# A two-layer hybrid encoder on Trainium2: the scan's output decay factors are loaded with its other loads, and four out-projection steps are written behind the last third's splits

## The chip, the cores and the metric

The kernel runs on one core of one Trainium2 chip, as one program. The metric is the device time of one execution in microseconds (us); the time of a kernel is the median of its runs. One core has a matrix engine (TensorE, PE; its weight loads are listed apart as PEld), a vector engine (VectorE, DVE), a scalar engine (ScalarE, ACT), GpSimd (POOL), and SyncE (SP), which here only issues transfers (DMAs). Each engine works through its own instructions in the order in which they stand, and waits where one needs what another engine or a transfer has not delivered. On-chip data lies in tiles; a pool of tiles under one tag has a fixed number of buffers, and a new tile waits until the last user of its buffer is done. Results of TensorE lie in PSUM banks until another engine has read them.

## The reference

Two layers, 1040 tokens (1024 and 16 meta tokens) of width 1024. Each layer: RMSNorm, one input projection to four groups of mixers (pooling, 2-D Fourier, a bidirectional state-space scan called SSD, attention) and their gates, one output projection, and the residual. The change lies in the scan and in the output projection of its group. The scan, cut to its core:

```python
def ssd_direction(xh, dt, a, bm, cm):
    ...
    da = (dt * a).reshape(b, nc, CHUNK, SSD_GROUPS, r).transpose(0, 1, 3, 4, 2)
    cs = jnp.cumsum(da, axis=-1)
    seg = cs[..., :, None] - cs[..., None, :]
    lmat = jnp.exp(jnp.where(lower, seg, -jnp.inf))
    cb = jnp.einsum("bclgn,bcsgn->bcgls", cc, bc)
    y_diag = jnp.einsum("bcgrls,bcsgrp->bclgrp", cb[:, :, :, None] * lmat, xdt)
    decay_to_end = jnp.exp(cs[..., -1:] - cs)
    chunk_states = jnp.einsum("bclgn,bcgrl,bclgrp->bcgrpn", bc, decay_to_end, xdt)
    ...
    _, prev = lax.scan(step, h0, (chunk_states, chunk_decay))
    y_off = jnp.einsum("bclgn,bcgrpn,bcgrl->bclgrp", cc, prev, jnp.exp(cs))
    return (y_diag + y_off).reshape(b, lp, nh, p)

def ssd_mixer(...):
    ...
    y = (y_fwd + y_bwd)[:, META_PAD:] + d_skip.astype(jnp.float32)[:, None] * xh
    y = y.reshape(b, n, W_SSD) * jax.nn.silu(z.astype(jnp.float32))
    return rmsnorm(y, norm_w).astype(out_dtype)
```

The kernel works with chunks of 104 tokens (QC), so 10 chunks (NQ) for a layer. The factors exp(cs) in `y_off` are what the kernel keeps under the name `ecd`; the cumulative sums for `lmat` are under `csd`.

## The kernel before

All is written as generators that yield after each piece, and a `weave` takes from several of them in proportion, so that the order on each engine is the order in which the pieces were written. Tokens are cut into three thirds of about 348, 346 and 346 columns (the last layer leaves the meta tokens out: 332, 346, 346; chunks 0, 1 and 2 in `ssd_fin` and `outproj`; "third" below, so as not to mix them with the scan's chunks).

The forward part of the scan is `ssd_fwd`. For scan chunk q, `prepare(q)` (P0 to P9 below) loads two broadcast tiles of cumulative sums, `rf` and `rb` (L868, L869, 338 KB each), from the pool `bb` with NBB = 5 buffers; the masks' products are L880 and L881 on VectorE; eight times L883 on VectorE and an Exp on ScalarE make the decays; eight times L887 on ScalarE and L888 on VectorE add the backward part; L889 on GpSimd multiplies both into `rb`. `finish(q)` (F0 to F9) takes a tile `e` from the pool `big`, loads the output decay factors into it with two transfers from `ecd` (L897), multiplies the products with the backward and forward states into it (L900, L903 on VectorE from PSUM; the matmuls are L825), updates the state (`ssd_state`: L808 on VectorE, L811 on TensorE, L817 on GpSimd, L818 on VectorE), adds both directions (L908 on GpSimd), does the products within the chunk (L914, 16 matmuls), adds them (L915) and writes y with the skip (four L917 on VectorE). The order is P0, P1, F0, P2, F1 and so on to P9, F8, F9: `prepare` runs one chunk ahead.

Where a third is complete, `ssd_fin` multiplies it with the gate z (loaded in L945; L950 on VectorE), sums the squares (L952 on ScalarE, L954 on VectorE) and yields; behind that yield come the sum over partitions on TensorE (L957), the root (L142 to L145) and the scaling (L961 on VectorE). `ssd_parts` then splits y into a high and a low part (L128 on ScalarE, L129 on VectorE), the two operands of the three-matmul products (L132 to L134). The same `split` is used on weights (`wl<-wr,wh`).

The scan is woven with other work: its first FW = 17 pieces with steps of the output projection of the attention group, its last 5 with `tail((0, 1))`, the out-projection of the scan's own group for thirds 0 and 1. That has 16 steps (8 output tiles d by 2 thirds; k0 to k15 below). A step loads the residual (`sms<-hd`, L338), runs 12 matmuls into PSUM `psmm`, adds the result to the residual on VectorE (L352), and stores it (L353). In this stage `psmm` has two banks. TW = 20 stands for 16 steps, so the weave writes them at four to a piece of the scan. Behind it comes `rest`, the same for the last third: its splits, and 8 steps. In the last layer `rest` runs alone; in the first it is woven with the next layer's input norm. SyncE issues all loads and stores named here, in order.

Of the kernel before, what the change touches and what calls it, by code (L numbers as in the profile page):

```python
# [52 lines left out]
def hybrid_trunk(ctx: ExitStack, tc: tile.TileContext, io, out, depth=DEPTH):  # L53
    nc = tc.nc
# [15 lines left out]
    nc.vector.memset(ones, 1.0)  # L70
    epst = const.tile([128, 1], F32, name="epst")
    nc.vector.memset(epst, EPS)
    FW, TW = 17, 20
    NBIG, NBB = 30, 5
    WB = (4, 5)
    PB, KB, NPF, NACC = 2, 3, 14, 4
    SPARE = (('xx', 'xx', 'mm'), ('sc', 'sc', 'mm'), ('xx', 'mm', 'xx'), ('xx', 'sc', 'xx'))
# [19 lines left out]
    def big(dt=F32):  # L97
        return bigp.tile([128, SLOT], dt, name=nm("big"), tag="big", bufs=NBIG)
# [758 lines left out]
    def ssd_fwd(l, s):  # L857
# [5 lines left out]
        def prepare(q):  # L863

            qs = slice(q * QC, (q + 1) * QC)
            tok = s.tok[q]
            rf, rb = vr(bb()[:QC]), vr(bb()[:QC])
            nc.sync.dma_start(rf, s.csd[q, 0].partition_broadcast(QC))  # L868
            nc.sync.dma_start(rb, s.csd[q, 1].partition_broadcast(QC))  # L869
            px, bt = ssd_tok(s, q)  # L870
            xx = big()
            xt, xw = xx[:QC, :512], xx[:QC, 512:1024]
            nc.scalar.copy(xt, px[:QC])
            pc = ps("xx")
            for g in range(2):
                nc.tensor.matmul(pc[:QC, g * QC:(g + 1) * QC], s.xbc[4 + g][:, qs], s.xbc[6 + g][:, qs], start=True, stop=True)
            cfb = phase["p"].tile([128, 4 * QC], F32, name=nm("cfb"), tag="cfb", bufs=1)[:QC].rearrange("p (g t) -> p g t", t=QC)
            cf, cb = cfb[:, 0:2], cfb[:, 2:4]
            pcv = pc[:QC, :2 * QC].rearrange("p (g t) -> p g t", t=QC)
            nc.vector.tensor_tensor(cf, pcv, mf.unsqueeze(1).broadcast_to([QC, 2, QC]), op=ALU.mult)  # L880
            nc.vector.tensor_tensor(cb, pcv, mb.unsqueeze(1).broadcast_to([QC, 2, QC]), op=ALU.mult)  # L881
            for r in range(8):
                nc.vector.scalar_tensor_tensor(rf[:, r], rb[:, r], s.gap[:, q, r:r + 1], rf[:, r], op0=ALU.add, op1=ALU.min)  # L883
                nc.scalar.activation(rf[:, r], rf[:, r], AF.Exp, bias=tok[:, r:r + 1])
            for r in range(8):
                g = (r % 4) // 2
                nc.scalar.activation(rb[:, r], cb[:, g], AF.Copy, scale=tok[:, 136 + r:137 + r])  # L887
                nc.vector.scalar_tensor_tensor(rb[:, r], cf[:, g], tok[:, 104 + r:105 + r], rb[:, r], op0=ALU.mult, op1=ALU.add)  # L888
            nc.gpsimd.tensor_tensor(rb, rb, rf, op=ALU.mult)  # L889
            ready[q] = (xt, xw, bt, rb)  # L890

        def finish(q, st):
            qs = slice(q * QC, (q + 1) * QC)
            xt, xw, bt, rb = ready.pop(q)
            e = vr(big())
            for a in range(2):
                nc.sync.dma_start(e[64 * a:64 * a + 64].rearrange("p (i j) t -> p i j t", i=2), s.ecd[q, :, 4 * a:4 * a + 4].partition_broadcast(64))  # L897
            if q < NQ - 1:
                pb = ssd_off(s, q, s.sb[q], "sc")
                nc.vector.tensor_tensor(e[:, 4:8], pb.rearrange("p (j t) -> p j t", t=QC), e[:, 4:8], op=ALU.mult)  # L900
            if q > 0:
                pf = ssd_off(s, q, st, "pv")
                nc.vector.tensor_tensor(e[:, 0:4], pf.rearrange("p (j t) -> p j t", t=QC), e[:, 0:4], op=ALU.mult)  # L903
            new = None
            if q < NQ - 1:
                new = ssd_state(s, 0, q, xt, bt, st, xw, s.sf[:, 512 * (q % 2):512 * (q % 2) + 512])
            if 0 < q < NQ - 1:
                nc.gpsimd.tensor_tensor(e[:, 0:4], e[:, 0:4], e[:, 4:8], op=ALU.add)  # L908
            y = e[:, 4:8] if q == 0 else e[:, 0:4]
            pd = ps("xx")  # L910
            for h in range(8):
                j, a = h // 2, h % 2
                r = 4 * a + j
                nc.tensor.matmul(pd[64 * a:64 * a + 64, j * QC:(j + 1) * QC], xt[:, h * 64:h * 64 + 64], rb[:, r], start=True, stop=True)  # L914
            nc.vector.tensor_tensor(y, y, pd[:, :4 * QC].rearrange("p (j t) -> p j t", t=QC), op=ALU.add)  # L915
            for j in range(4):
                nc.vector.scalar_tensor_tensor(s.y[j][:, qs], s.xbc[j][:, qs], vec(l, V_DS + j), y[:, j], op0=ALU.mult, op1=ALU.add)  # L917
            return new
# [3 lines left out]
        for q in range(NQ + 1):  # L922
# [7 lines left out]
            if q:  # L930
                st = finish(q - 1, st)
                ci = next((i for i, (c0, cw) in enumerate(CH) if (q - 1) * QC < c0 + cw <= q * QC), None)
                if ci is not None:
                    norm = ssd_fin(l, s, ci)
                    next(norm)
                yield
        next(norm, None)
        yield

# [38 lines left out]
    def run(*gens):  # L978
        for g in gens:
            for _ in g:  # L980
                pass
# [41 lines left out]
    for l in range(depth):  # L1023
# [59 lines left out]
        stage(bwd, 5, FB[7])  # L1083
        hsrc = by_rows(out, NM) if last else hidden()
        sink = None if last else []
        tail = lambda chunks: outproj(l, s, 2, lambda: ssd_parts(s, chunks), d1, hsrc, chunks, sink=sink)
        fwd = ssd_fwd(l, s)
        n = 48 - FB[6] - FB[7]
        stage(islice(fwd, FW), FW, n)
        run(weave((fwd, 22 - FW), (tail((0, 1)), TW)))  # L1090
        scope.close()
        rest = tail((2,))
        if last:
            run(rest)
        else:
# [109 lines left out]
```

## Time and profile before

| | before |
|---|---|
| three runs, median (lowest to highest) | 2136.37 us (2135.49 to 2142.13) |
| the profiled execution | 2144.23 us |
| its span in the profile | 2142.5 us |
| mean granted clock of TensorE | 0.969 |
| scan of layer 0, forward, up to F9 | about 825 to 1062 us of the span |
| forward scan of layer 1, up to F9 | up to 2114 us of the span |

The page of a profile lists engines with busy time and share, then groups of instructions. A group or a row of the timeline reads: start, duration, engine, line, operation, output tile, inputs, and in brackets how long the engine stood idle before it and what released it. A window's row lists the busy time of each engine in a stretch of time, the granted clock of TensorE (1.00 is full), and the share of the transfer engines in use. Times in rows count from the start of the span. A transfer is named by its tiles (`big<-ecd`). Records of successive instructions overlap a little, by some 0.08 us on VectorE.

### The profile page before, as it was taken

What the parts mean: (1) busy time and instruction counts of PE and PEld (TensorE: products, weight loads), DVE (VectorE), ACT (ScalarE), POOL (GpSimd) and SP (SyncE); (2) the same over time, 40 slices, a digit from 0 to 9 for tenths busy, and PEclk for the clock granted to TensorE, in tenths of its full rate; (3) what the DMA queues carried; (4) which work ended last, traced back from release to release, by engine and by line L of the source; (5) the groups of instructions that cost most, each with busy time, mean ns of one, the idle gap of its engine ahead of it and who ended that gap; (6) DMA issues with size and microseconds to landing.
All of it is one profiled execution on the core that took longest, in us unless ns stands there. A gap on an engine that the chain in (4) does not pass through costs nothing.

```text
span 2142.5 us, 33401 instructions
## 1 busy us (share of the span) xinstructions
PE 2007.5 (94%) x11880; PEld 1756.2 (82%) x11880; DVE 1398.6 (65%) x2785; ACT 1012.6 (47%) x2191; POOL 464.2 (22%) x465
## 2 busy tenths in 40 slices
PE   6999999999999898888889999999999998979888
PEld 5898988688899568877779988877888995878878
DVE  5575547767664455689795655476675635476996
ACT  5534344453542546356464344435534433463652
POOL 2012122031110210245230221221311103012550
PEclk9999999999999999999999999998999999988999
DMA  4322222123233477676643221212223344776666
GB/s 138 99 74 62 64 63 57 43 76 97 91 127 104 135 210 246 193 187 191 169 123 116 66 67 54 73 44 72 68 98 102 117 129 127 241 217 180 175 184 195
DMA packets 164605, 261.01 MB, mean 122 GB/s; under 512 B 20878, under 2 KB 113618, under 8 KB 164438
## 3 DMA queue, kind: packets, MB, share of 16 engines
q1 hardware_dynamic: 161782, 249.55, 38.7%
q0 software_dynamic: 2656, 9.33, 1.8%
q8 instruction: 93, 1.52, 0.3%
q14 instruction: 74, 0.61, 0.1%
HBM read 182.91 MB, written 71.67 MB: 119 GB/s over the span
## 4 chain that ended last, share of the span: by engine, by line
PE 68%; DVE 14%; DMA 9%; ACT 4%; issue 3%; POOL 2%; SPq 1%; DVEq 0%; POOLq 0%; ACTq 0%
PE psmm L132 11%; PE psmm L133 10%; PE psmm L134 10%; PE pspv L678 6%; PE psy L132 5%; PE psy L133 5%; PE psy L134 5%; PE psy L655 2%; PE psy L626 2%; PE psy L656 2%; DMA hd<-sms 2%; DVE bb L883 1%; PE pssc L655 1%; DMA big<-ecd 1%; PE pssc L626 1%
## 5 line engine op out<-in xcount | busy, mean ns | idle before, releaser
L132 PE MATMUL psmm<-big,wh 128*128 128x346 f32 (+2 forms) x1920 | 645.5, 337 | 42.0 <-DVE sms L352 19.2
L133 PE MATMUL psmm<-big,wh 128*128 128x346 f32 (+2 forms) x1920 | 633.8, 330 | 7.6 <-DVE big L129 4.7
L134 PE MATMUL psmm<-big,wl 128*128 128x346 f32 (+2 forms) x1920 | 628.2, 327 | 1.3 <-DVE wl L129 1.3
L132 PEld LDWEIGHTS psmm<-big,wh 128*128 128x128 f32 x1920 | 370.8, 193 | 88.0 <-issue 29.3
L133 PEld LDWEIGHTS psmm<-big,wh 128*128 128x128 f32 x1920 | 371.0, 193 | 17.8 <-DVE big L129 7.2
L134 PEld LDWEIGHTS psmm<-big,wl 128*128 128x128 f32 x1920 | 371.3, 193 | 4.5 <-DVE wl L129 2.4
L668 POOL TENSOR_TENSOR acc<-acc,pf 116x346 f32<-116x346 f32 (+5 forms) x216 | 222.9, 1044 | 701.2 <-ACT pf L658 557.4
L128 ACT CAST wh<-wr 128x512 fp32r<-128x512 f32 (+1 forms) x236 | 145.2, 616 | 268.6 <-PE psmm L133 205.8
L129 DVE TENSOR_TENSOR wl<-wr,wh 128x512 fp32r<-128x512 f32 x232 | 168.4, 730 | 126.6 <-ACT wh L128 125.2
L132 PE MATMUL psy<-big,wh 128*128 128x346 f32 (+2 forms) x672 | 221.8, 330 | 1.1 <-ACT big L128 0.6
L133 PE MATMUL psy<-big,wh 128*128 128x346 f32 (+2 forms) x672 | 217.7, 324 | 3.1 <-DVE big L188 2.0
L134 PE MATMUL psy<-big,wl 128*128 128x346 f32 (+2 forms) x672 | 216.8, 323 | 0.0
L678 PE MATMUL pspv<-pf,vt 116*64 116x346 f32 (+5 forms) x864 | 168.8, 469 | 0.0
L658 ACT ACTIVATE pf<-psy 116x346 f32<-116x346 f32 (+4 forms) x288 | 125.3, 457 | 87.0 <-PE psy L656 84.8
L668 DVE TENSOR_TENSOR acc<-acc,pf 116x346 f32<-116x346 f32 (+5 forms) x120 | 106.7, 889 | 71.5 <-ACT pf L658 51.0
L627 DVE TENSOR_REDUCE mx<-psy 116x1 f32<-116x346 f32 (+3 forms) x272 | 132.7, 511 | 18.5 <-PE psy L626 18.0
L132 PEld LDWEIGHTS psy<-big,wh 128*128 128x128 f32 x672 | 127.2, 189 | 13.3 <-issue 7.6
L133 PEld LDWEIGHTS psy<-big,wh 128*128 128x128 f32 x672 | 127.0, 189 | 6.9 <-DVE big L188 3.1
L134 PEld LDWEIGHTS psy<-big,wl 128*128 128x128 f32 x672 | 127.0, 189 | 0.8
L678 PEld LDWEIGHTS pspv<-pf,vt 116*64 116x64 f32 (+1 forms) x864 | 59.4, 137 | 62.5 <-issue 26.7
L655 PE MATMUL psy<-big,big 128*116 128x346 f32 (+4 forms) x288 | 96.2, 336 | 0.9 <-DVE mx L627 0.8
L627 DVE TENSOR_REDUCE mx<-pssc 128x1 f32<-128x346 f32 (+3 forms) x136 | 69.8, 513 | 41.7 <-PE pssc L626 40.0
(293 smaller groups left out, 3326.7 us busy)
## 6 DMA issues: line engine op xcount, KB each, us to landing
wr<-w SPq DMA_DIRECT2D x248, 256.0 KB
sms<-hd SPq DMA_DIRECT2D x112, 173.0 KB
hd<-sms SPq DMA_DIRECT2D x96, 173.0 KB
bb<-csd SPq DMA_DIRECT2D x40, 338.0 KB
md<-big SPq DMA_DIRECT2D x24, 520.0 KB
gd<-sms SPq DMA_DIRECT2D x64, 173.0 KB
big<-gd SPq DMA_DIRECT2D x16, 520.0 KB
big<-md SPq DMA_DIRECT2D x16, 520.0 KB
```

The lines of the kernel that those rows point to most:

```text
L128: nc.scalar.copy(hi, src)
L129: nc.vector.tensor_tensor(lo, src, f(hi), op=ALU.subtract)
L132: nc.tensor.matmul(out_ps, ah, bh, start=start, stop=False)
L133: nc.tensor.matmul(out_ps, ah, bl, start=False, stop=False)
L134: nc.tensor.matmul(out_ps, al, bh, start=False, stop=stop)
L626: nc.tensor.matmul(p[:qn, :cw], s1[e][:, q0:q0 + qn], k1[:, c0:c0 + cw], start=True, stop=True)
L627: nc.vector.tensor_reduce(mx[:qn, q, e, ci:ci + 1], p[:qn, :cw], axis=AX.X, op=ALU.max)
L655: nc.tensor.matmul(p[:n, :cw], k1[:, k0:k0 + n], s1[e][:, cs], start=True, stop=False)
L656: nc.tensor.matmul(p[:n, :cw], k3[0:65, k0:k0 + n], q2[e][0:65, cs], start=False, stop=True)
L658: nc.scalar.activation(pf[:n, :cw], p[:n, :cw], AF.Exp, scale=0.125)
L668: eng.tensor_tensor(accs[c0, e][:n, :cw], accs[c0, e][:n, :cw], pf[:n, :cw], op=ALU.add)
L678: nc.tensor.matmul(hold["pv"][64 * e:64 * e + 64, :cw], s.vt[:n, k, v, :], pfs[e][:n, :cw], start=(k == 0), stop=(k == len(KTS) - 1))
```

## The change

There are three edits. First, `e` is taken from the pool `bb` and loaded in `prepare(q)`, right behind the loads of `rf` and `rb`, instead of in `finish(q)` from `big`; `bb` gets 7 buffers instead of 5 (three tiles a chunk instead of two). Second, `ssd_fwd` yields twice more, with no work, ahead of the last third's norm. Third, of the 16 steps of `tail((0, 1))` only the first 12 (TL) are woven with the last 7 pieces of the scan; then `ssd_parts` of the last third is written, then the remaining 4 steps (`run(front)`), and then `rest`, which takes the splits already written. The number of matmuls, products and transfers is the same.

Lines of the functions move by 3 and by 2: L880 becomes L883, L883 L886, L888 L891, L889 L892, L945 L947, L950 L952, L954 L956, L957 L959, L961 L963; L900 to L917 keep their numbers, and the load of e is L872 instead of L897.

```diff
@@ -70,8 +70,8 @@
     nc.vector.memset(ones, 1.0)
     epst = const.tile([128, 1], F32, name="epst")
     nc.vector.memset(epst, EPS)
-    FW, TW = 17, 20
-    NBIG, NBB = 30, 5
+    FW, TL = 17, 12
+    NBIG, NBB = 30, 7
     WB = (4, 5)
     PB, KB, NPF, NACC = 2, 3, 14, 4
     SPARE = (('xx', 'xx', 'mm'), ('sc', 'sc', 'mm'), ('xx', 'mm', 'xx'), ('xx', 'sc', 'xx'))
@@ -867,6 +867,9 @@
             rf, rb = vr(bb()[:QC]), vr(bb()[:QC])
             nc.sync.dma_start(rf, s.csd[q, 0].partition_broadcast(QC))
             nc.sync.dma_start(rb, s.csd[q, 1].partition_broadcast(QC))
+            e = vr(bb())
+            for a in range(2):
+                nc.sync.dma_start(e[64 * a:64 * a + 64].rearrange("p (i j) t -> p i j t", i=2), s.ecd[q, :, 4 * a:4 * a + 4].partition_broadcast(64))
             px, bt = ssd_tok(s, q)
             xx = big()
             xt, xw = xx[:QC, :512], xx[:QC, 512:1024]
@@ -887,14 +890,11 @@
                 nc.scalar.activation(rb[:, r], cb[:, g], AF.Copy, scale=tok[:, 136 + r:137 + r])
                 nc.vector.scalar_tensor_tensor(rb[:, r], cf[:, g], tok[:, 104 + r:105 + r], rb[:, r], op0=ALU.mult, op1=ALU.add)
             nc.gpsimd.tensor_tensor(rb, rb, rf, op=ALU.mult)
-            ready[q] = (xt, xw, bt, rb)
+            ready[q] = (xt, xw, bt, rb, e)
 
         def finish(q, st):
             qs = slice(q * QC, (q + 1) * QC)
-            xt, xw, bt, rb = ready.pop(q)
-            e = vr(big())
-            for a in range(2):
-                nc.sync.dma_start(e[64 * a:64 * a + 64].rearrange("p (i j) t -> p i j t", i=2), s.ecd[q, :, 4 * a:4 * a + 4].partition_broadcast(64))
+            xt, xw, bt, rb, e = ready.pop(q)
             if q < NQ - 1:
                 pb = ssd_off(s, q, s.sb[q], "sc")
                 nc.vector.tensor_tensor(e[:, 4:8], pb.rearrange("p (j t) -> p j t", t=QC), e[:, 4:8], op=ALU.mult)
@@ -934,6 +934,8 @@
                     norm = ssd_fin(l, s, ci)
                     next(norm)
                 yield
+        yield
+        yield
         next(norm, None)
         yield
 
@@ -1083,13 +1085,16 @@
         stage(bwd, 5, FB[7])
         hsrc = by_rows(out, NM) if last else hidden()
         sink = None if last else []
-        tail = lambda chunks: outproj(l, s, 2, lambda: ssd_parts(s, chunks), d1, hsrc, chunks, sink=sink)
+        tail = lambda chunks, parts: outproj(l, s, 2, parts, d1, hsrc, chunks, sink=sink)
         fwd = ssd_fwd(l, s)
         n = 48 - FB[6] - FB[7]
         stage(islice(fwd, FW), FW, n)
-        run(weave((fwd, 22 - FW), (tail((0, 1)), TW)))
+        front = tail((0, 1), lambda: ssd_parts(s, (0, 1)))
+        run(weave((fwd, 24 - FW), (islice(front, TL), TL)))
         scope.close()
-        rest = tail((2,))
+        ym = ssd_parts(s, (2,))
+        run(front)
+        rest = tail((2,), lambda: ym)
         if last:
             run(rest)
         else:
```

What moves on the engines, at three places. First SyncE, the tail of layer 0's scan: e of the last chunk (`big_10708`) before the change, between stores of the residual (`hd_8851`, `hd_8852`) and loads of weights (`wr`). A row is the line, the operation, the output and input tile with its buffer number, and the shape.

```order
L205 DMA wr_11043<-w 128x512
L205 DMA wr_11099<-w 128x512
L897 DMA big_10708<-ecd_3642 64x2x416
L353 DMA hd_8851<-big_10688 128x348
L353 DMA hd_8852<-big_10688 128x346
L897 DMA big_10708<-ecd_3642 64x2x416
L205 DMA wr_11131<-w 128x512
```

The same tile after the change (`bb_10441`), among the loads and stores of the residual (`sms<-hd`, `hd<-sms`) of the last attention steps:

```order
L868 DMA bb_10437<-csd_3641 104x832
L338 DMA sms_10182<-hd_5734 128x346
L338 DMA sms_10201<-hd_5735 128x346
L869 DMA bb_10438<-csd_3641 104x832
L947 DMA z_10608<-gd_6603 128x4x346
L353 DMA hd_5731<-sms_10182 128x346
L353 DMA hd_5732<-sms_10201 128x346
L338 DMA sms_10299<-hd_5733 128x348
L205 DMA wr_10818<-w 128x512
L338 DMA sms_10318<-hd_5734 128x346
L872 DMA bb_10441<-ecd_3642 64x2x416
```

The load has moved ahead of the whole tail, to the other loads of its chunk, and in front of residual loads and stores of attention steps.

Second VectorE, the tail of layer 1's scan, before: the evictions of the steps (L352) stand close together ahead of F9's first product (L903).

```order
L352 TENSOR_TENSOR sms_21509<-sms_21509,psmm_21511 128x332
L352 TENSOR_TENSOR sms_21526<-sms_21526,psmm_21528 128x346
L129 TENSOR_TENSOR wl_21775<-wr_21772,wh_21774 128x512
L352 TENSOR_TENSOR sms_21549<-sms_21549,psmm_21551 128x332
L352 TENSOR_TENSOR sms_21566<-sms_21566,psmm_21568 128x346
L129 TENSOR_TENSOR wl_21798<-wr_21795,wh_21797 128x512
L903 TENSOR_TENSOR big_21583<-pspv_21586,big_21583 128x416
```

The last two L352 above are those of steps k8 and k9. After the change, from the eviction of step k3 on:

```order
L352 TENSOR_TENSOR sms_21449<-sms_21449,psmm_21451 128x346
L915 TENSOR_TENSOR bb_21104<-bb_21104,psy_21435 128x416
L129 TENSOR_TENSOR wl_21548<-wr_21545,wh_21547 128x512
L818 TENSOR_TENSOR big_19757<-big_19757,pspv_21428 128x512
L917 SCALAR_TENSOR_TENSOR big_19073<-big_19073,vecs,bb_21104 128x104
L917 SCALAR_TENSOR_TENSOR big_19074<-big_19074,vecs,bb_21104 128x104
L917 SCALAR_TENSOR_TENSOR big_19075<-big_19075,vecs,bb_21104 128x104
L917 SCALAR_TENSOR_TENSOR big_19076<-big_19076,vecs,bb_21104 128x104
L129 TENSOR_TENSOR wl_21588<-wr_21585,wh_21587 128x512
L903 TENSOR_TENSOR bb_21320<-pspv_21466,bb_21320 128x416
L129 TENSOR_TENSOR wl_21643<-wr_21640,wh_21642 128x512
```

Evictions of the first four steps (k0 to k3) now stand ahead of the end of F8, and no other L352 stands among the rest of F8 and F9. The next one, that of k4, follows 24 rows behind that of k3.

Third VectorE, the same tail, around the last third's squares. Before (L954 sums the squares, L143 is the root's first step, behind the norm sum on TensorE; the L352 are of k10, k11 and k12):

```order
L954 TENSOR_TENSOR sms_21610<-sms_21610,smn_21618 128x346
L129 TENSOR_TENSOR wl_21821<-wr_21818,wh_21820 128x512
L954 TENSOR_TENSOR sms_21610<-sms_21610,smn_21622 128x346
L352 TENSOR_TENSOR sms_21631<-sms_21631,psmm_21633 128x332
L352 TENSOR_TENSOR sms_21648<-sms_21648,psmm_21650 128x346
L143 SCALAR_TENSOR_TENSOR smn_21711<-psy_21705,smn_21711 128x346
L352 TENSOR_TENSOR sms_21671<-sms_21671,psmm_21673 128x332
```

After (the sum is L956; the L352 are of k4 to k8):

```order
L956 TENSOR_TENSOR sms_21490<-sms_21490,smn_21494 128x346
L129 TENSOR_TENSOR wl_21735<-wr_21732,wh_21734 128x512
L956 TENSOR_TENSOR sms_21490<-sms_21490,smn_21498 128x346
L352 TENSOR_TENSOR sms_21511<-sms_21511,psmm_21513 128x332
L956 TENSOR_TENSOR sms_21490<-sms_21490,smn_21502 128x346
L352 TENSOR_TENSOR sms_21528<-sms_21528,psmm_21530 128x346
L352 TENSOR_TENSOR sms_21551<-sms_21551,psmm_21553 128x332
L352 TENSOR_TENSOR sms_21568<-sms_21568,psmm_21570 128x346
L129 TENSOR_TENSOR wl_21775<-wr_21772,wh_21774 128x512
L352 TENSOR_TENSOR sms_21591<-sms_21591,psmm_21593 128x332
L143 SCALAR_TENSOR_TENSOR smn_21614<-psy_21608,smn_21614 128x346
```

Between the last sum of squares and the root there stood two steps; now there are four, and seven steps in place of four follow the norm sum on TensorE.

## The prediction

> **What bounds the kernel now.** I read the page first, then busy time in windows of the scan and of the work behind it, then the waits of TensorE (PE) and VectorE (DVE) there. The page says whose time counts:
>
> ```profile
> PE 2007.5 (94%) x11880; PEld 1756.2 (82%) x11880; DVE 1398.6 (65%) x2785; ACT 1012.6 (47%) x2191; POOL 464.2 (22%) x465
> ```
>
> TensorE sets the span, so a gain has to come out of TensorE's waits or of its slow clock. In the changed stage it is more mixed. Columns of the windows: length, then busy us and count of PE, PEld, DVE, ACT, POOL, then granted clock, DMA share, GB/s.
>
> ```profile
> 960.00:980.00 20.00, 16.68 (x101) 14.53 (x101) 20.00 (x46) 15.51 (x40) 10.40 (x9) 0.93 0.70 180
> 1000.00:1020.00 20.00, 17.93 (x109) 16.82 (x109) 18.24 (x40) 12.90 (x36) 11.40 (x10) 0.83 0.69 195
> 2020.00:2040.00 20.00, 17.32 (x119) 15.72 (x118) 19.64 (x43) 13.62 (x33) 11.68 (x11) 0.91 0.56 153
> 2060.00:2080.00 20.00, 16.50 (x103) 15.10 (x102) 19.32 (x43) 12.88 (x37) 10.79 (x10) 0.83 0.72 194
> 1056.00:1062.00 6.00, 0.22 (x2) 0.00 (x0) 5.69 (x15) 2.35 (x5) 0.35 (x1) 0.75 0.47 128
> 1062.00:1066.00 4.00, 3.88 (x12) 3.40 (x13) 1.57 (x5) 2.26 (x6) 0.00 (x0) 0.52 0.63 149
> 2108.00:2114.00 6.00, 2.80 (x18) 2.51 (x17) 5.75 (x15) 2.25 (x5) 0.00 (x0) 0.97 0.76 251
> 2114.00:2117.00 3.00, 3.00 (x9) 2.52 (x10) 0.59 (x3) 1.53 (x3) 0.00 (x0) 0.50 0.77 228
> ```
>
> In the scan VectorE is busy 18.2 to 20.0 of 20 us while TensorE has holes and a clock of 0.83 to 0.93: VectorE is the bound there. At the scan's end (1056 to 1062, 2108 to 2114) TensorE stands while VectorE finishes, and then runs at half clock. Those two holes are what the held-back steps aim at. Their waits, with TensorE's short operations around them:
>
> ```profile
> 1046.55 1.10 PE L811 MATMUL pspv<-big,smq 104*128 104x256 f32 x4 [1.31 <-DVE big L903]
> 1062.12 1.52 PE L957 MATMUL psy<-sms,ones 128*128 128x346 f32 x2 [5.90 <-DVE sms L954]
> 2104.80 1.04 PE L825 MATMUL pspv<-big,big 128*128 128x104 f32 x8
> 2105.76 0.93 PE L914 MATMUL psxx<-bb,big 104*64 104x104 f32 x16
> 2113.80 1.52 PE L957 MATMUL psy<-sms,ones 128*128 128x346 f32 x2 [3.20 <-DVE sms L954]
> ```
>
> So 1.31 + 5.90 us in layer 0 and 3.20 us in layer 1. Behind each long one lies half clock: 4.0 us at 0.52 and 3.0 us at 0.50, about 1.9 and 1.5 us lost.
>
> **Part 1: e is loaded two chunks ahead.** VectorE's waits for it, and what GpSimd (POOL) and SyncE did there:
>
> ```profile
> 1000.78 0.59 DVE L900 TENSOR_TENSOR big<-pssc,big 128x416 f32<-128x416 f32 x1 [1.56 <-DMA big<-ecd]
> 1045.31 0.59 DVE L900 TENSOR_TENSOR big<-pssc,big 128x416 f32<-128x416 f32 x1 [2.37 <-DMA big<-ecd]
> 1051.50 0.58 SPq L897 DMA_DIRECT2D big<-ecd  x1
> 1055.83 0.59 DVE L903 TENSOR_TENSOR big<-pspv,big 128x416 f32<-128x416 f32 x1 [4.08 <-DMA big<-ecd]
> 2010.49 1.06 POOL L908 TENSOR_TENSOR big<-big 128x416 f32<-128x416 f32 x1
> 2011.59 0.59 DVE L915 TENSOR_TENSOR big<-big,psxx 128x416 f32<-128x416 f32 x1 [1.42 <-POOL big L908]
> ```
>
> All of these but the last name a DMA that SyncE issued late, behind stores of the residual; F9's second half was issued at 1051.50 and used at 1055.83. After the change no use of e waits. What is late next differs. In layer 0's scan (1000.78) VectorE goes on at once with ready work: I take 0.9 of the 1.56 us (nothing to 1.56 are the ends; GpSimd's add, 1.06 us as in the row of 2010.49, follows e and takes part back). In layer 1's scan VectorE's next wait is for that add, itself behind GpSimd's queue, so an earlier e saves about nothing. The waits at 1045.31 and 1055.83 belong to the tail, summed below as a whole. Three tiles of bb a chunk on seven buffers instead of two on five cost no instruction, but move the slot waits: rf of chunk k now waits for the last L917 of chunk k-3, where it waited for its L914 matmuls, and e of chunk k for the L914 of chunk k-2. From L914's start at 2105.76 to the end of its L917 (2108.91 + 1.04, below) are 4.2 us, from L914's end 3.3 us. SyncE works in order, and behind the waiting DMA stand residual loads (L338) and stores (L353) of the attention steps. I set this against the just-in-time e loads that no longer stand in front of the tail's stores: nothing net, between -3 us and the loss of the second rival.
>
> **Part 2: fewer steps woven in, four held back.** A step is 12 matmuls. The tail's ends in both layers (first mask product of the last chunk, L880; eviction of the last of the 16 steps, L352), the pace of matmuls at full clock, and VectorE's pieces:
>
> ```profile
> 1029.93 0.36 DVE L880 TENSOR_TENSOR cfb<-psy,ct 104x208 f32<-104x208 f32 x1
> 1073.93 0.50 DVE L352 TENSOR_TENSOR big<-sms,psmm 128x346 f32<-128x346 f32 x1
> 2086.37 0.36 DVE L880 TENSOR_TENSOR cfb<-psy,ct 104x208 f32<-104x208 f32 x1
> 2123.73 0.52 DVE L352 TENSOR_TENSOR sms<-sms,psmm 128x346 f32<-128x346 f32 x1
> 2126.00:2136.00 10.00, 10.00 (x65) 10.00 (x64) 4.83 (x9) 1.34 (x3) 0.00 (x0) 1.00 0.73 201
> 1048.57 0.67 DVE L818 TENSOR_TENSOR big<-big,pspv 128x512 f32<-128x512 f32 x1
> 2107.60 0.58 DVE L903 TENSOR_TENSOR big<-pspv,big 128x416 f32<-128x416 f32 x1
> 2108.29 0.59 DVE L915 TENSOR_TENSOR big<-big,psxx 128x416 f32<-128x416 f32 x1
> 2108.91 1.04 DVE L917 SCALAR_TENSOR_TENSOR big<-big,vecs,big 128x104 f32<-128x104 f32 x4
> 2109.87 1.79 DVE L950 TENSOR_TENSOR big<-big,z 128x346 f32<-128x346 f32 x4
> 2111.58 1.13 DVE L954 TENSOR_TENSOR sms<-sms,smn 128x346 f32<-128x346 f32 x2
> 2112.63 0.69 DVE L129 TENSOR_TENSOR wl<-wr,wh 128x512 fp32r<-128x512 f32 x1
> 2092.58 2.00 POOL L889 TENSOR_TENSOR bb<-bb,bb 104x832 f32<-104x832 f32 x1 [8.66 <-DVE bb L888]
> 2124.16 0.51 DVE L129 TENSOR_TENSOR big<-big,big 128x346 fp32r<-128x346 f32 x1
> 2093.85 2.32 DVE L129 TENSOR_TENSOR wl<-wr,wh 128x512 fp32r<-128x512 f32 x1
> ```
>
> A step is 12 x 10/65 = 1.85 us. I count from T, the start of L880. Before, the 16th step is evicted at T + 44.5 us in layer 0 (1074.43) and T + 37.9 in layer 1 (2124.25). After, by the order of the change:
>
> - The second step (k1) is done at about T; before at T + 2. Steps k2 to k15 then take 14 x 1.85 = 25.9 us.
> - TensorE's scan work: L811 1.0, two L825 of 1.0 and 0.5 (the last chunk has one direction only), two L914 of 0.9, the norm sum 0.5 at full clock (its 1.52 us is at half clock): 4.8 us.
> - F9's L914 now stands only two to three steps behind P9, and waits for L892 (L889 before) on GpSimd. That ends 8.2 us after T (2092.58 + 2.00 - 2086.37); TensorE has k2, k3, some of k4 and F8's L825 and L914 to do, 6.5 to 7 us: a wait of 1.3.
> - L811 of F8 needs VectorE's L808, which stands where L892 and L908 run on GpSimd. The last two rows above show a neighbour with the same fate: L129 took 2.32 us instead of 0.69 beside L889. I put 1.7 us there (the stretch of that row, nothing if L808 gets through), and 0.6 for F9's L825 behind the next.
> - Then the costly one. Only two PSUM banks serve the steps, so the step after next waits for L352. Between L352 of k3 and L352 of k4 VectorE now has 23 instructions: two L915, five L129, one L818, eight L917, one L903, four L952, two L956: 1.18 + 3.45 + 0.67 + 2.08 + 0.58 + 1.79 + 1.13 = 10.9 us, less some 0.08 us by which neighbours overlap at 13 joints: 9.8. Meanwhile TensorE has L811, the rest of k4, half an L825 and k5: some 4.6 us. **It waits 9.8 - 4.6 = 5.2 us.** Before, the same stretch (L352 of k9 to k10) held two L129, L903, L915, four L917, four L950, three L954: 7.0 - 0.6 = 6.4 us, and it ended in the norm sum's 3.20.
> - Behind 5.2 us the clock is halved again, as behind 3.20 and 5.90: 1.9 us, the larger of the two losses above.
> - The norm chain behind the sum (from 2113.80 to 2124.67, where the row of 2124.16 ends the last split: 10.9 us) is covered by 7 held-back and late steps, 13 us: no wait there, as there was none before in layer 1.
>
> Sum: 25.9 + 4.8 + 1.3 + 1.7 + 0.6 + 5.2 + 1.9 + 0.5 for the last eviction = 41.9 us behind T. Against 44.5 that gains 2.6 in layer 0, against 37.9 it loses 4.0 in layer 1. The hole has moved from behind the scan into it, where it is as deep: VectorE has the same work to do before the norm, and the fewer steps around it leave it in one block. T itself comes earlier by 0.9 (layer 0, part 1) and by 0.4 in each layer, since an L352 (0.5 us) that stood in front of it goes behind. Together -2.6 + 4.0 - 0.9 - 0.8 = -0.3 us. The two `yield`s alone cost no instruction. The profiled execution took 2144.23 us (its span 2142.5), so it would take 2143.9; the median of the runs is 2136.37, 7.9 lower, and less 0.3 gives **2136 us**.
>
> **A rule of the Trainium skill beside the clock term.** Its page "TensorE: Matmul & The Clock Gate", section "Part 1: The HAM clock gate (the "warmup" mystery)", says that the clock falls to half after at least one idle window of about 3.4 us and returns after about 3.4 us of work. The half clock after 5.90 us agrees; that after 3.20 us is a little below the stated window. By the page the 5.2 us wait would cost an estimated 1.7 us (half of 3.4) in place of 1.9, and the sum would be 0.4 us lower over two layers.
>
> **The rivals.**
>
> *Faster: the waits lie over one another.* While TensorE waits for GpSimd, VectorE goes on, so the 1.3, 1.7 and 0.6 us may be eaten out of the 9.8 us block instead of standing ahead of it; then 5.2 us is the whole wait of a layer, spread in pieces too short to halve the clock. That removes 3.6 + 1.9 us a layer, 11 us: 2125. For it: VectorE's own total is unchanged, and e no longer stops it for 2.37 and 4.08 us in layer 0. Against it: F8's L915 and F9's L903 are in that block and need L914 and L825, which stand behind the very waits.
>
> *Slower: SyncE's queue.* A bb slot comes free 3.3 us later (above), and SyncE stands at the load that waits for it. In layer 0's scan (880 to 1050 for SyncE, to 1030 for VectorE; total us, times, longest) it stood at such loads before, and VectorE waited for loads:
>
> ```profile
> SPq L868 <- POOL bb L889: 3.7, 3, 1.9
> DVE sms L352 <- DMA sms<-hd: 4.9, 5, 1.8
> DVE bb L883 <- DMA bb<-csd: 2.5, 1, 2.5
> ```
>
> If the lead is used up, the csd load and the residual loads behind it come later, and VectorE, full in the scan, cannot catch up. It decides when a load that was in time has under 3.3 us to spare. VectorE waited 4.9 + 2.5 = 7.4 us for such loads in a layer; if that grows by half, 3.7 us a layer, 7.4 in both give 2144. For it: loads come just in time already. Against it: waits for L868 are three in a scan, and the e loads come off the tail.
>
> *It does nothing where it says:* the waits for e were not what ended the scan. This is the forecast itself in layer 1, at 2011.59.
>
> **How the numbers follow.** A measurement of this kernel tells 0.3%, 6.4 us, from no change. Forecast (no change, 2130 to 2143): 0.45; the first rival, faster: 0.31; the second, slower: 0.24. The unknown costs are 1.7 (L808) and 0.6 in each layer, 0.9 against 1.56, and SyncE's -3; singly they stay inside the forecast's own range. The whole range takes in both rivals with 2 us beyond each: 2123 to 2146.
>
> **What would show it.** Right: no wait for ecd at the products that were L900 and L903; a wait of 4 to 6 us of TensorE for L352 between F9's L914 and the norm sum, with a clock near 0.5 behind it; none at the norm sum. Wrong: that wait under 2 us (first rival); L883 or L900 waiting for a DMA from csd or ecd in mid-scan, or a longer scan from P3 on (second rival). It would also be wrong if the four held-back steps no longer met weights and residual in time, which SyncE now issues earlier.

## The result: slower by 0.7%, and the profile after

| | before | after |
|---|---|---|
| median of 7 runs (lowest to highest) | 2138.86 us (2134.20 to 2146.87) | 2152.78 us (2149.78 to 2159.29) |
| ratio, 95% interval | 1 | 1.0071 (1.0050 to 1.0092) |
| profiled execution (its span) | 2144.23 us (2142.5) | 2154.47 us (2152.7) |

The prediction was 2136 us and no change; the measured time lies above its range. The two profiled executions differ by 10.2 us, the medians by 13.9. On the page of after the engines have as many instructions as before and about the same busy time:

```profile
PE 1999.7 (93%) x11880; PEld 1755.6 (82%) x11880; DVE 1395.2 (65%) x2785; ACT 1014.1 (47%) x2191; POOL 458.3 (21%) x465
```

So the time is waiting. Windows of after, first the four of the scan, then TensorE's hole and what follows it, in layer 0 and in layer 1 (columns as before):

```profile
960.00:980.00 20.00, 18.53 (x116) 17.32 (x115) 17.33 (x47) 16.43 (x41) 9.34 (x9) 0.83 0.55 150
1000.00:1020.00 20.00, 15.64 (x105) 14.48 (x105) 16.92 (x43) 12.71 (x36) 9.57 (x9) 0.91 0.76 222
2020.00:2040.00 20.00, 17.80 (x134) 16.84 (x136) 20.00 (x45) 15.43 (x40) 9.89 (x9) 1.00 0.63 176
2060.00:2080.00 20.00, 15.31 (x99) 14.19 (x99) 19.23 (x44) 13.16 (x37) 10.39 (x10) 0.91 0.67 196
1048.00:1052.00 4.00, 0.29 (x2) 0.00 (x1) 3.98 (x11) 2.40 (x5) 0.35 (x1) 1.00 0.80 255
1052.00:1056.00 4.00, 3.52 (x14) 3.52 (x15) 1.55 (x4) 0.00 (x0) 0.00 (x0) 0.66 0.71 214
2105.00:2109.00 4.00, 0.00 (x0) 0.00 (x0) 4.00 (x12) 2.17 (x5) 0.00 (x0) 0.87 0.80 256
2109.00:2113.00 4.00, 3.57 (x13) 3.57 (x14) 1.23 (x3) 0.00 (x0) 0.00 (x0) 0.50 0.52 160
```

Two things are to be seen. In layer 0's scan VectorE, the bound there, is now busy 17.3 and 16.9 of 20 us, where it was busy 20.0 and 18.2; in layer 1's windows it is as busy as before. And the hole behind the scan is now in it, nearly as deep as was forecast (waits of 4.19 and 4.54 us, where 5.2 was the sum's), with the clock at 0.66 and 0.50 behind it.

What VectorE waits for in layer 0 stands in the waits from 790 to 1045 (total us, times, longest). SyncE at its loads of rf, rb and e, and VectorE for csd, before:

```profile
SPq L868 <- POOL bb L889: 3.7, 3, 1.9
SPq L869 <- PE psxx L914: 2.8, 1, 2.8
SPq L869 <- POOL bb L889: 2.2, 2, 1.2
DVE bb L883 <- DMA bb<-csd: 2.5, 1, 2.5
```

and after:

```profile
SPq L872 <- POOL bb L892: 11.9, 6, 3.2
SPq L869 <- DVE big L917: 4.4, 2, 3.0
SPq L872 <- DVE bb L900: 2.3, 1, 2.3
DVE bb L886 <- DMA bb<-csd: 12.3, 6, 3.5
```

With the smaller rows of the same lines SyncE stands 22.9 us at these loads, before 9.4; VectorE waits 12.3 us for cumulative sums, before 2.5. SyncE's waits as a whole did not grow, though: over all its lines, stores (L353) and residual loads (L338) above all, they are 164.5 us in this stretch, before 164.0. What grew is the idle time of VectorE behind it, from 58.9 to 67.5 us. One link of it in the timeline of after:

```profile
967.29 1.96 POOL L892 TENSOR_TENSOR bb<-bb,bb 104x832 f32<-104x832 f32 x1 [3.73 <-DVE bb L891]
969.27 0.59 SPq L872 DMA_DIRECT2D bb<-ecd  x1
974.72 0.51 SPq L868 DMA_DIRECT2D bb<-csd  x1
980.41 0.40 SPq L869 DMA_DIRECT2D bb<-csd  x1
985.30 0.33 DVE L886 SCALAR_TENSOR_TENSOR bb<-bb,gap,bb 104x104 f32<-104x104 f32 x1 [3.21 <-DMA bb<-csd]
```

The first half of e is issued the moment L892 of the chunk before is done (967.29 + 1.96 = 969.25), after a wait of 2.8 us; the next chunk's rf and rb come behind it, and VectorE stands 3.21 us for them. The lateness is not e's alone: between 969.5 and 981 SyncE also stood 6.3 us at stores that waited for GpSimd's L350, the last of them (3.8 us) just ahead of rb.

### The profile page after: what moved, and what is told of

Same layout as the page of the kernel before. It is cut to its first block, busy times and chain, and to the rows that moved or that the text cites. A ratio compares the mean times of both kernels' runs of the same rounds, so it can differ in the third digit from the quotient of the medians.

```text
span 2152.7 us, 33396 instructions
## 1 busy us (share of the span) xinstructions
PE 1999.7 (93%) x11880; PEld 1755.6 (82%) x11880; DVE 1395.2 (65%) x2785; ACT 1014.1 (47%) x2191; POOL 458.3 (21%) x465
## 4 chain that ended last, share of the span: by engine, by line
PE 64%; DVE 14%; DMA 12%; ACT 5%; issue 3%; POOL 1%; SPq 1%; DVEq 0%; POOLq 0%; ACTq 0%
PE psmm L132 10%; PE psmm L133 10%; PE psmm L134 10%; PE pspv L678 6%; PE psy L132 4%; PE psy L133 4%; PE psy L134 4%; DMA hd<-sms 3%; PE psy L655 2%; PE psy L626 2%; PE psy L656 2%; DVE bb L886 2%; DMA sms<-hd 2%; DMA big<-gd 1%; PE pssc L655 1%
## 5 line engine op out<-in xcount | busy, mean ns | idle before, releaser
L129 DVE TENSOR_TENSOR wl<-wr,wh 128x512 fp32r<-128x512 f32 x232 | 163.4, 708 | 126.7 <-ACT wh L128 125.6
L678 PEld LDWEIGHTS pspv<-pf,vt 116*64 116x64 f32 (+1 forms) x864 | 58.9, 136 | 61.5 <-issue 26.1
```

What stands on the lines that cost most here:

```text
L129: nc.vector.tensor_tensor(lo, src, f(hi), op=ALU.subtract)
L678: nc.tensor.matmul(hold["pv"][64 * e:64 * e + 64, :cw], s.vt[:n, k, v, :], pfs[e][:n, :cw], start=(k == 0), stop=(k == len(KTS) - 1))
```

## The experiments

Fourteen kernels ran, each against the kernel before on the same chip. Theory Q is the second rival of the prediction with a mechanism of its own: SyncE waits at the head of its queue for a buffer of bb, and what stands behind comes late. Theories H and T put the loss into the tail. The measured values together; "SyncE" is its total wait at the loads of rf, rb and e in layer 0 and in layer 1 (790 to 1045 and 1845 to 2090), "F4 to end" the time from the fifth L915 of layer 1 to the span's end:

| run | ratio to before (95%) | SyncE, us | F4 to end, us |
|---|---|---|---|
| before | 1 | 9.4, 7.7 | 115.2 |
| the change | 1.0071 (1.0050 to 1.0092) | 22.9, 25.3 | 121.9 |
| e_loads_only | 1.0024 (1.0006 to 1.0041) | 26.3, 26.4 | 114.5 |
| hold_back_only | 1.0033 (1.0017 to 1.0050) | 10.5, 7.4 | 122.6 |
| change_8_buffers | 1.0134 (1.0104 to 1.0165) | 31.6, 35.1 | 122.0 |
| e_loads_8_buffers | 1.0072 (1.0047 to 1.0097) | 31.0, 33.2 | 115.8 |
| e_early_from_big | 1.0003 (0.9990 to 1.0016) | 6.8, 10.9 | 115.4 |
| hold_back_split | 1.0017 (1.0001 to 1.0033) | 10.3, 6.1 | 118.6 |
| hold_none | 1.0046 (1.0032 to 1.0060) | 9.7, 7.9 | 119.0 |
| change_e_from_big | 1.0038 (1.0023 to 1.0053) | 6.6, 10.6 | 121.4 |
| change_e_big_split | 1.0016 (1.0004 to 1.0028) | 7.6, 11.0 | 119.3 |
| e_big_old_tail_split | 1.0041 (1.0026 to 1.0056) | 8.7, 10.7 | 121.0 |
| e_big_split_hold2 | 1.0018 (1.0005 to 1.0031) | 7.8, 11.0 | 118.3 |

e_on_gpsimd_queue, e_loads_10_buffers and before_big_28 stand in their own paragraphs.

**The two halves apart.** e_loads_only is the first edit alone, on the old tail:

```diff
-    NBIG, NBB = 30, 5
+    NBIG, NBB = 30, 7
...
+            e = vr(bb())
+            for a in range(2):
+                nc.sync.dma_start(e[64 * a:64 * a + 64]..., s.ecd[q, ...])
```

hold_back_only is the second and third edit alone:

```diff
-    FW, TW = 17, 20
+    FW, TL = 17, 12
...
+        yield
+        yield
         next(norm, None)
...
-        run(weave((fwd, 22 - FW), (tail((0, 1)), TW)))
+        front = tail((0, 1), lambda: ssd_parts(s, (0, 1)))
+        run(weave((fwd, 24 - FW), (islice(front, TL), TL)))
...
+        ym = ssd_parts(s, (2,))
+        run(front)
+        rest = tail((2,), lambda: ym)
```

> The decay factors e are loaded with the chunk's other loads into the scan's pool of 7 buffers; the tail of the scan is that of the kernel before (16 steps woven at once, no extra yields, splits of the last third behind them). Theory Q (queue: with 7 buffers the load of e waits on SyncE for L892 of the chunk before, and the next cumulative sums stand behind it): the scan from P3 to P9 is as slow as in the changed kernel, 102 to 105 us against 98 before, VectorE waits 3 to 8 us a scan for csd; 5 to 8 us above the kernel before in the scans, less 2 to 4 us in layer 0's tail where the waits for e go: 2 to 6 us slower than before. Theory H (the hole moved into the scan's tail is the whole loss): 0 to 4 us faster than before.

> Only the other half of the change: 12 of the 16 steps woven, two yields, splits of the last third ahead of the last 4 steps; e is still loaded late into the pool big, 5 buffers in bb. Theory Q: scans from P3 to P9 last 98 us as before, and the loss is only that of layer 1's tail (about 5 to 7 us against a gain or loss of 2 in layer 0): 2 to 8 us slower than before. Theory H: the whole 10 to 15 us are here.

Both halves cost: 0.24% and 0.33%, together about 12 us against the change's 15 (0.71% of 2138.86). Theory H falls, since the first half costs without any change of the tail. The SyncE column splits along the first half, the last column along the second. What was expected of the scan from P3 to P9 also came: 102.5 and 101.5 us in e_loads_only, against 97.8 and 98.3 before. So did late cumulative sums: from F0 to F4 VectorE waits 2.6 and 1.1 us for csd there and 2.7 and 2.2 in the change, and not at all in the kernel before and in hold_back_only. VectorE's whole idle time from 790 to 1045 is 68.5 us in e_loads_only and 58.6 in hold_back_only, where it is 58.9 before.

**One buffer more.**

```diff
-    NBIG, NBB = 30, 7
+    NBIG, NBB = 30, 8
```

> The changed kernel with one buffer more in bb (8). By the order of releases e then takes a buffer that is free after F of three chunks before, and rf one that is free after L892 of two chunks before. Theory Q: waits of SyncE at the load of e fall from 10 to 12 us a scan to under 4, VectorE's waits for csd to under 3, the scan from P3 to P9 comes back to about 98 us, and 6 to 10 us of the loss go: 2142 to 2147 against 2139 before. Theory H: the time stays within 3 us of the changed kernel, 2150 to 2156.

> As e_loads_only (tail of the kernel before), with 8 buffers in bb. Theory Q: no late csd, and the waits for e are gone, so the time is at or below the kernel before, by 0 to 6 us. Theory H: the same as e_loads_only within 2 us.

Both missed, to the other side: 0.6% and 0.5% slower still. SyncE and VectorE in change_8_buffers, 790 to 1045:

```profile
SPq L868 <- POOL bb L892: 9.1, 4, 4.0
SPq L872 <- DVE big L917: 7.2, 3, 3.4
SPq L869 <- POOL bb L892: 6.5, 2, 5.2
DVE sms L352 <- DMA sms<-hd: 9.5, 7, 2.3
```

The buffer did not take SyncE's waits away but moved them: 31.6 us in place of 22.9, now at other loads, and what comes late behind them are the residual loads (9.5 us of VectorE's waiting, 4.9 before). In the program's order a load of chunk 2 had moved up some 70 places in SyncE's queue, since a buffer is now foreseen for it earlier. So the count of buffers is the wrong remedy. SyncE's sum and the time go up together, but that does not show that one makes the other: VectorE's wait for csd fell (3.3 us from 790 to 1045, 12.3 in the change), and the scan from P3 to P9 is shorter than in the change (101.2 and 99.0 us, against 105.1 and 102.2). In the profiled execution of change_8_buffers 8.0 of the 11.3 us by which it is longer than that of the change have come up before layer 0's P0. Why the eighth buffer costs 0.6% stays open.

**The same early load, another pool.**

```diff
-            e = vr(bb())
+            e = vr(big())
```

with NBB = 5 and the old tail.

> As e_loads_only (e loaded in prepare beside rf and rb, old tail), but its tile comes from the pool big as in the kernel before, and bb keeps its 5 buffers, so rf and rb take the same buffers as before. Theory Q (SyncE is held up by the wait for a buffer of bb, and the cumulative sums behind it come late): the time from F0 to F4 (first to fifth L915) goes back from 54 us to 48 to 50 in both layers, VectorE's wait for csd there under 2 us, and the total is 3 to 8 us below e_loads_only, at or below the kernel before. Theory D (the load two chunks ahead, by its traffic and its place in the queue, costs the time, whatever buffer it takes): F0 to F4 stays at 52 to 55 us and the total within 2 us of e_loads_only.

1.0003: no loss is left that can be told, with e still loaded in `prepare`. The ratio is 0.21% below e_loads_only, and the intervals overlap, so this run alone would not show the difference; the same edit in the whole change, below, takes off 0.33%. SyncE's rows of this run, 790 to 1045:

```profile
SPq L868 <- POOL bb L892: 2.5, 2, 1.5
SPq L869 <- POOL bb L892: 2.4, 2, 1.3
```

Its waits are back at 6.8 and 10.9 us, VectorE waits for no csd from F0 to F4, and VectorE's idle time from 790 to 1045 is 57.1 us. That speaks against theory D, that the early load itself costs. By the stretches that had been named it is less clear: F0 to F4 came out at 50.5 and 52.0 us, not all of the way to 48, and P3 to P9 at 100.1 and 101.1. But F0 is earlier there, and from P0 to F4 it is 94.5 and 96.0 us, against 94.4 and 96.3 before and 97.4 and 97.1 in e_loads_only. One rival is left: with tiles from big the e loads of the first three chunks stand later in SyncE's queue (in layer 0 at its 447th to 452nd transfer, in e_loads_only at the 318th to 444th), so the two kernels differ ahead of the scan too. The load gains nothing either: no wait for e is left, and the time is that of the kernel before.

**e issued by GpSimd.**

```diff
-                nc.sync.dma_start(e[64 * a:64 * a + 64]...
+                nc.gpsimd.dma_start(e[64 * a:64 * a + 64]...
```

> As e_loads_only with 7 buffers, but the two loads of e are issued by GpSimd instead of SyncE, so that SyncE's queue has no wait of e in it. Theory Q: F0 to F4 48 to 51 us, csd in time; what is left is what GpSimd loses by issuing (its L350 and L908 later): total 0 to 6 us below e_loads_only. Theory D: F0 to F4 stays at 52 us or more, total as e_loads_only or slower.

1.0109 (1.0091 to 1.0127): theory Q's time did not come, and "as e_loads_only or slower", which was theory D's, did. It does not separate the two all the same: rf and rb still take buffers that e held, so the waits for a buffer stayed on SyncE, and it stood 38.5 us at them in layer 0, more than in any run of the table:

```profile
SPq L869 <- DVE big L917: 17.6, 5, 4.5
SPq L868 <- POOL bb L892: 11.8, 2, 6.3
```

**The hole in the tail.** hold_back_split puts one yield between F9 and the last third's squares, into hold_back_only.

```diff
                 if ci is not None:
+                    if q == NQ:
+                        yield
                     norm = ssd_fin(l, s, ci)
...
-        run(weave((fwd, 24 - FW), (islice(front, TL), TL)))
+        run(weave((fwd, 25 - FW), (islice(front, TL), TL)))
```

hold_none holds nothing back:

```diff
-    FW, TL = 17, 12
+    FW, TL = 17, 16
```

> hold_back_only with one more yield, between F9 and the squares of the last third, so that a step can be written there and its L352 stands inside VectorE's long block. Theory T (TensorE's wait of 4 to 4.5 us for L352 and the half clock behind it are what the held-back steps cost in layer 1): the wait becomes two of 1 to 2.5 us or less, layer 1 from F4 to the end shrinks from 122 us by 2 to 4, the total is 2 to 6 us below hold_back_only. Rival U (the loss lies behind the norm, in late residual loads and in the last third's steps): the same total as hold_back_only within 2 us.

> hold_back_only with all 16 steps woven into the last 7 pieces and none held back behind the splits. Theory T: more L352 stand among F8 and F9, the hole there shrinks to under 2 us, but the norm sum's wait comes back (3 to 6 us): 0 to 4 us below hold_back_only, and at or 0 to 5 us above the kernel before. Rival U: as hold_back_only, since the late loads stay.

TensorE's first matmul behind the hole, layer 1, in hold_back_split:

```profile
2097.47 0.43 PE L132 MATMUL psmm<-big,wh 128*128 128x346 f32 x1 [2.54 <-DVE sms L352]
```

In hold_back_only the same row reads:

```profile
2094.47 0.65 PE L132 MATMUL psmm<-big,wh 128*128 128x332 f32 x1 [4.03 <-DVE sms L352]
```

The wait is 1.5 us shorter, layer 1 from F4 to the end 4.0 us shorter of the 7.4 that hold_back_only adds there, and the ratio 0.16% lower: as theory T expected, but with intervals that overlap by half. By these numbers the hole is about half of what the second half costs; the rest isn't told apart. hold_none missed: its wait fell to 2.16 us, but it is 0.46% slower than the kernel before, with no step held back. So spreading the steps over 7 pieces costs by itself; whether holding four of them back pays anything, 0.33% against 0.46%, is inside the noise.

**The parts put together.** change_e_from_big is the whole change with e's tile from big and NBB = 5; change_e_big_split has the extra yield too; e_big_split_hold2 has TL = 14 besides; e_big_old_tail_split is e_early_from_big with the extra yield alone, and `(fwd, 23 - FW)` in its weave. The edits are those shown above.

> The whole change, but e's tile comes from the pool big and bb keeps 5 buffers (e is still loaded in prepare). Theory Q+T (the loss is the sum of SyncE's waits for a buffer of bb, 5 us, and of the moved hole, 7 us): only the hole is left, as in hold_back_only: 0.2 to 0.5% slower than before, 4 to 10 us; no wait of VectorE for csd over 1.5 us in F0 to F4; k3 to k4 about 10.5 us apart in layer 1. Rival V (the two halves need each other, early e makes the held-back steps pay): at or below the kernel before. Rival D: 0.6% or more slower, as the change.

> As change_e_from_big with a yield between F9 and the squares of the last third. Theory Q+T: as hold_back_split, 0 to 0.3% slower than before; TensorE's wait for L352 in layer 1 under 3 us. If the hole were all of part 2 and splitting it removed it whole, 0 to 3 us faster than before.

> e early from big, all 16 steps woven as before, nothing held back, with the yield between F9 and the squares alone. Theory T: the block of VectorE is cut by an L352, TensorE's wait at the norm sum (1.75 us in layer 1 in e_early_from_big) goes or moves: 0 to 4 us faster than e_early_from_big and than before. Otherwise: the same within 2 us.

> As change_e_big_split with 14 of the 16 steps woven and 2 held back. Theory T: more evictions stand among F8 and F9, so the hole is smaller than with 12: 0 to 4 us faster than change_e_big_split, within 3 us of the kernel before.

change_e_from_big costs 0.38%, as hold_back_only does (0.33%) and 0.33% less than the change, so the halves add and rival V falls. TensorE's hole is all there (k3 to k4 are 10.6 us apart by the rows of L352), SyncE's waits are not. The split gives a like share back (0.22%), with a wait of 1.51 us left. Two held back instead of four change nothing that can be told. e_big_old_tail_split missed: 15 of the 16 steps then stand ahead of the norm sum, one behind it, and TensorE stands behind that one instead, for the last third's splits:

```profile
2121.09 0.58 PE L132 MATMUL psmm<-big,wh 128*128 128x346 f32 x2 [3.18 <-ACT big L128]
```

That is the wait which the held-back steps were written for; in the kernel before, where four steps stand there by the weave alone, it does not arise. No version beat the kernel before.

**Ten buffers, with a control.**

```diff
-    NBIG, NBB = 30, 7
+    NBIG, NBB = 28, 10
```

> As e_loads_only and e_loads_8_buffers, with 10 buffers in bb and 28 in big to make room. With 8 buffers SyncE stood 5 to 6 us at rb of chunk 2 for L892 of chunk 0; with 10 all loads of chunks 0 to 2 find a fresh buffer. Theory Q (waits for a buffer at the head of SyncE's queue cost the time): SyncE's waits at loads of rf, rb and e fall under 8 us a scan, VectorE's waits for csd under 2 us in F0 to F4, the total is 3 to 8 us below e_loads_only, within 3 us of e_early_from_big. Theory E (more loads issued early cost by themselves, in the stage ahead of the scan): L423 to F0 183 us or more as with 8 buffers, the total at 8 us or more above the kernel before.

> The control: the kernel before with 28 buffers in big instead of 30. If e_loads_10_buffers differs from before because of the two buffers fewer, it shows here; expected the same as before within 3 us.

2234.30 and 2233.46 us, both 1.0448 times the kernel before: two buffers fewer in big cost 97 us by themselves, against the control's expectation. Against that control ten buffers cost nothing, but SyncE still waited (one load 12.9 us for L892), and the scan's start is late in both, so this neither supports Q nor speaks against it. Theory E, that loads issued ahead of the scan cost by themselves, stays open with it.

## Why the prediction was wrong, by its own steps

The signs that it named for being right all came: VectorE's waits for ecd went from 9.0 us in the two layers to none, TensorE waits 4.19 and 4.54 us for L352 with the clock near half behind it, and it does not wait at the norm sum. The sign of the second rival, waits for csd in mid-scan, came as well. Two terms of the sum failed, one in each part; the two halves of the change cost 0.24% and 0.33%.

**The step that failed in part 1: "nothing net" for SyncE's queue.** Two things were wrong in it. First which buffer a load waits for. I had buffers of bb come round in a fixed turn, so that e of chunk k would wait for the L914 of chunk k-2. Handing them out in the order in which they come free, gone through by hand for seven buffers, gives rf the buffer of rb three chunks back, rb that of e three chunks back, and e the buffer of rf of the chunk just before, free only after its L892; the waits of after name just these (L872 for L892, L869 for L917). So e, meant to be two chunks early, is tied to the middle of the chunk before, and holds back what stands behind it in SyncE's queue. Second the price. I set a possible loss against the e loads leaving the tail and took zero; the waits went from 9.4 to 22.9 us in layer 0 and from 7.7 to 25.3 in layer 1. e_loads_only shows 0.24%, about 5 us, where the sum had a gain of 0.9. The second rival had the right place and sign, and 7.4 us for it.

The last chunk's start T was to come 1.3 us earlier in layer 0. It came 3.4 later (1033.33 against 1029.93), and 3.3 later in layer 1. These are places in two single executions, and hold everything ahead of them; the ratio of e_loads_only is the firmer figure.

**The step that failed in part 2: its net, -2.6 + 4.0 - 0.8 = +0.6 us.** hold_back_only shows 0.33%, about 7 us. The costly wait was seen rightly; what failed is the gain of layer 0, and what lies behind the 16th eviction. Timeline of after, VectorE's T and the 16th eviction in both layers, and between them TensorE's waits, and VectorE's L808 and GpSimd's L892 in layer 1:

```profile
1033.33 0.36 DVE L883 TENSOR_TENSOR cfb<-psy,ct 104x208 f32<-104x208 f32 x1
1052.48 0.43 PE L132 MATMUL psmm<-big,wh 128*128 128x348 f32 x1 [4.19 <-DVE big L352]
1068.54 0.40 PE L132 MATMUL psmm<-big,wh 128*128 128x348 f32 x1 [2.19 <-ACT big L128]
1076.46 0.52 DVE L352 TENSOR_TENSOR big<-sms,psmm 128x346 f32<-128x346 f32 x1 [0.33 <-PE psmm L134]
2089.70 0.36 DVE L883 TENSOR_TENSOR cfb<-psy,ct 104x208 f32<-104x208 f32 x1
2094.98 1.98 POOL L892 TENSOR_TENSOR bb<-bb,bb 104x832 f32<-104x832 f32 x1 [7.45 <-DVE bb L891]
2095.32 3.11 DVE L808 TENSOR_TENSOR big<-big,big 104x256 f32<-104x256 f32 x2
2097.01 0.57 PE L914 MATMUL psxx<-bb,big 104*64 104x104 f32 x6 [0.43 <-POOL bb L892]
2098.58 1.10 PE L811 MATMUL pspv<-big,smq 104*128 104x256 f32 x4 [1.00 <-DVE big L808]
2109.43 0.64 PE L132 MATMUL psmm<-big,wh 128*128 128x332 f32 x1 [4.54 <-DVE sms L352]
2131.88 0.52 DVE L352 TENSOR_TENSOR sms<-sms,psmm 128x346 f32<-128x346 f32 x1 [1.85 <-DMA sms<-hd]
2135.67 0.52 DVE L352 TENSOR_TENSOR sms<-sms,psmm 128x346 f32<-128x346 f32 x1 [2.68 <-DMA sms<-hd]
```

From T to the end of the 16th eviction are 43.7 us in layer 0 and 42.7 in layer 1; 41.9 was the sum. That it came so near is in part luck, as its terms did not: the wait for L352 is 4.19 and 4.54 us (5.2), those for L892 and L808 are 0.43 and 1.00 in layer 1 and none in layer 0 (1.3 and 1.7), and the 0.6 for the next L825 is none. In their place layer 0 has two things that the sum lacked: half clock at T (a window below), and the wait of 2.19 us behind the norm sum (row of 1068.54), where seven steps were to cover all. L808 itself took 3.11 us for two beside L892. In another chunk of the kernel before two took 0.74 us beside L889, but there it was L889 that was stretched, to 3.66 us:

```profile
2071.75 0.74 DVE L808 TENSOR_TENSOR big<-big,big 104x256 f32<-104x256 f32 x2
2071.67 3.66 POOL L889 TENSOR_TENSOR bb<-bb,bb 104x832 f32<-104x832 f32 x1 [3.05 <-DVE bb L888]
1033.00:1036.00 3.00, 3.00 (x12) 3.00 (x12) 2.35 (x9) 1.61 (x5) 0.00 (x0) 0.50 0.16 60
```

So in these rows the overlap cost now the one engine, now the other. The last row is the window at T in layer 0 of after, at half clock. Against before the stretch from T is -0.8 us in layer 0 (-2.6 forecast) and +4.8 in layer 1 (+4.0).

**A term that was missing**: what follows the 16th eviction. The step behind it waited 2.68 us for its residual (row of 2135.67), and from the eviction's end to the span's end are 20.3 us, against 18.25 before: +2.0. With it part 2 is -0.8 + 4.8 + 2.0 = +6.0 us by the traces. (That layer 1's T, tail and end, 3.3 + 4.8 + 2.0, add up to the profiled difference holds by construction.) The held-back steps need not be the reason for the late residual: in hold_none, which holds none back, 21.1 us follow the 16th eviction, and two later evictions wait 1.76 and 2.63 us for their residual. The cause of this term stays open.

**The first rival** (waits that lie over one another) came in part: the three small waits are nearly gone, but the wait for L352 stood almost whole and the clock was halved behind it. The gain of layer 0 in the forecast, 3.9 us with T, set against layer 1's loss, made the sum look like no change: it was the term with the least support.

## What to carry to other kernels

A load that is made early waits early: on an engine that issues in order, look for the buffer that it will get, by the order in which buffers come free, and for what is queued behind it, before counting what it saves. Five buffers that suit two tiles a round say little on seven for three; here a pool in which the load hardly waits left no loss of the early load that could be told, and one buffer more made it larger. And steps moved behind a wait leave a hole where they stood: with two banks the bound is how far apart two evictions stand on the engine that makes them.

## What the runs showed of the hardware

The clock can fall after shorter waits than the 5.90 and 3.20 us of the kernel before. Windows behind a wait of 2.54 us in hold_back_split and behind 1.75 us in e_early_from_big:

```profile
2097.40:2101.00 3.60, 3.53 (x13) 3.54 (x14) 0.85 (x3) 0.20 (x1) 0.00 (x0) 0.55 0.55 169
```

```profile
2101.40:2105.00 3.60, 3.56 (x21) 3.35 (x22) 1.86 (x5) 1.54 (x3) 0.00 (x0) 1.00 0.66 218
```

Half clock behind the one, full clock behind the other. The length of the wait does not decide it alone. Windows behind a wait of 2.16 us in hold_none (before its row of 2098.28) and behind 2.15 us in the changed kernel (before its row of 2088.14), with TensorE busy all of the 4 us ahead of either:

```profile
2098.20:2101.80 3.60, 3.52 (x15) 3.52 (x16) 1.28 (x4) 0.00 (x0) 0.00 (x0) 0.61 0.52 170
```

```profile
2088.10:2091.70 3.60, 3.56 (x23) 3.56 (x24) 3.60 (x13) 3.10 (x9) 0.00 (x0) 1.00 0.58 149
```

And behind waits of 3.36 us the clock was 0.53 in the changed kernel (from 1005.5) and 1.00 in change_e_from_big (from 1011.9). The Trainium skill, page "TensorE: Matmul & The Clock Gate", section "Part 1: The HAM clock gate (the "warmup" mystery)", gives an idle window of about 3.4 us; here waits of 2.16 and 2.54 us were enough in two runs, and one of 3.36 us was not in a third. In hold_back_split the half clock stayed though the wait became shorter. In change_e_big_split the clock is full behind the 1.51 us that are left (1.00 from 2100.0 to 2103.6), and there too only part of the loss came back, so the clock is not the whole reason.
